# Attention matmuls of one 128-block: 128 streamed columns in place of 256 padded ones

## The chip, the cores and the metric

The kernel runs on one core of a Trainium2 chip. The metric is the device time of one execution in microseconds, the median over several runs; less is better.

## The reference

A decoder trunk of two layers on one sequence of 512 tokens with 1024 features, in float32:

```python
for i in range(DEPTH):                       # 2 layers
    hn = rmsnorm(h, norm_mix_g[i])
    h = h + (even_mixer if i % 2 == 0 else odd_mixer)(hn, ...)
    hn = rmsnorm(h, norm_mlp_g[i])
    u = jnp.square(jax.nn.relu(hn @ w_mlp_up[i]))      # 1024 -> 4096
    h = h + u @ w_mlp_down[i]
    gate = jax.nn.sigmoid(rmsnorm(h, norm_ple_g[i]) @ w_ple_gate[i])
    h = h + (p[i] @ w_ple_proj[i]) * gate
return rmsnorm(h, final_norm_g)
```

The even layer has 8 stick-breaking heads of width 64 and 4 differential heads, each with two score maps and values of width 128. The odd layer has 16 heads of width 64 with dilated windows. All are causal: a query attends to keys at or before it. The change touches only the two products of attention, `scores = q k^T` and `out = weights v`.

## The kernel before

Tokens are kept along the free axis (512 columns), features along the 128 partitions. To keep float32 accuracy with the rounded type `F32R`, most operands are held as a rounded part and its remainder, and most products are done as three matmuls, `mm3` at L129 to L131: high x high, low weights x high, high weights x low. Each matmul loads 128 columns of weights (in the profile LDWEIGHTS on PEld) and streams the other operand (MATMUL on PE).

The mixer of a layer works on groups of heads. While the projections of the next group run on PE (`project`, `lin_units`), the attention of the current group is fed in by steps (`attend`, `step`, `interleave`). For a head and a query block `i` (128 queries, 4 blocks), a step does

- `scores` (L479): two matmuls at L484 and L485 into a tile `sc` of which there are two, over the keys 0 to `n`, with the queries as the weights; the second uses `klz`, the keys' low part;
- `soft` (L494), or sigmoids and a running product for stick-breaking (L554 to L564), on DVE and ACT;
- `transpose_in` (L506), three steps later: it transposes `i + 1` blocks of weights on PE (L510) and writes them to `pth` (rounded, ACT, L514) and `ptl` (remainder, DVE, L515).

When the four query blocks of a head are done, `combine` calls `pv` (L517), the value products: for each key block `j` two matmuls (three in differential heads), with the values as weights, streaming the attention weights of the queries from `P * j` on.

`pth` and `ptl` have 13 slots of 128 columns. Slot `3 * j + i` holds the weights of key block `j` and query block `i`, so those of key block `j` start at slot `4 * j` and end with slot `3 * j + 3`. Key block 3 has one query block, slot 12. Before the change its product streams slots 11 and 12, and slot 11 is kept at zero: it is cleared once in each layer by GpSimd (L367). Likewise the scores of query block 0 need 128 keys, and `scores` streams 256. The further 128 columns are not read by anything.

The order of the work on each engine is set by a scheduler from its own costs of the instructions and from the dependences, so a change of shapes can also move instructions. Tiles that are used in turn (`sc` 2, `tp` 2, `pv` 1) set what waits for what.

Of the kernel before, what the change touches and what calls it, by code (L numbers as in the profile page):

```python
# [12 lines left out]
F32 = mybir.dt.float32  # L13
# [6 lines left out]
P = 128  # L20
# [42 lines left out]
def trunk(  # L63
# [5 lines left out]
    nc = tc.nc  # L69
    uid = [0]  # L70

    def nm(s):
        uid[0] += 1
        return f"{s}_{uid[0]}"
# [21 lines left out]
    def ps(tag):  # L96
        return psum.tile([P, S], F32, tag=tag, name=nm(tag), bufs=PS_BUFS[tag])
# [262 lines left out]
    def mixer(layer, norm, nxt):  # L360
# [2 lines left out]
        NSLOT = 13  # L363
        pth = [mpool.tile([P, NSLOT, P], F32R, tag=f"pth{i}", name=nm("pth"), bufs=1) for i in range(2)]
        ptl = [mpool.tile([P, NSLOT, P], F32R, tag=f"ptl{i}", name=nm("ptl"), bufs=1) for i in range(2)]
        for t in pth + ptl:
            nc.gpsimd.memset(t[:, 11, :].bitcast(F32), 0.0)  # L367
        pt_i = [0]

        ahl = norm.parts()  # L370
# [107 lines left out]

        def scores(hd, i):  # L479
            q, kh, kl = hd  # L480
            n = max(256, P * (i + 1))
            sp = ps("sc")
            qs = slice(i * P, (i + 1) * P)
            nc.tensor.matmul(sp[:, 0:n], q[:, qs], kh[:, 0:n], start=True, stop=False)  # L484
            nc.tensor.matmul(sp[:, 0:n], q[:, qs], kl[:, 0:n], start=False, stop=True)  # L485
            return sp
# [7 lines left out]
        def soft(hd, bt, i):  # L494
            n = P * (i + 1)
            sp = scores(hd, i)
            e = t2k("e")
            mn, s, r = col("mn"), col("s"), col("r")
            nc.vector.tensor_tensor_reduce(  # L499
                e[:, 0:n], sp[:, 0:n], bt[:, 0:n][:, ::-1], op0=ALU.add, op1=ALU.min,  # L500
                scale=1.0, scalar=3e38, accum_out=mn)
            nc.scalar.activation(e[:, 0:n], e[:, 0:n], AF.Exp, scale=-1.0, bias=mn, accum_out=s)  # L502
            nc.vector.reciprocal(r, s)
            return e, r
# [12 lines left out]
        def pv(parts):  # L517
            op = ps("pv")
            nmm = len(parts) * QT
            c = 0  # L520
            for j in range(QT):
                s0, q0 = (11, 256) if j == 3 else (4 * j, P * j)
                for stat, pt in parts:
                    mov = pt[:, s0:3 * j + 4, :].rearrange("p a b -> p (a b)")
                    nc.tensor.matmul(op[:, q0:S], stat(j), mov, start=c == 0, stop=c == nmm - 1)  # L525
                    c += 1
            return op

        def attend(g, kind, v, heads):
# [6 lines left out]
            def weights(x, i):  # L536
                n = P * (i + 1)
                if kind == "diff":
                    if i == 0:
                        slot = 8 + 2 * (2 * (g - 2) + x)  # L540
                        bias[x] = [load_bias(slot + m) for m in range(2)]
                    e0, r0 = soft(heads[2 * x], bias[x][0], i)
                    e1, r1 = soft(heads[2 * x + 1], bias[x][1], i)
                    nc.vector.tensor_scalar(e1[:, 0:n], e1[:, 0:n], r1, neglam, op0=ALU.mult, op1=ALU.mult)
                    nc.vector.scalar_tensor_tensor(
                        e0[:, 0:n], e0[:, 0:n], r0, e1[:, 0:n], op0=ALU.mult, op1=ALU.add)
                    return e0
                if kind == "dil":
                    if i == 0:
                        bias[x] = load_bias(4 * g + x)  # L550
                    e, r = soft(heads[x], bias[x], i)
                    nc.vector.tensor_scalar(e[:, 0:n], e[:, 0:n], r, None, op0=ALU.mult)
                    return e
                sp = scores(heads[x], i)  # L554
                dg = slice(i * P, (i + 1) * P)
                nc.vector.tensor_tensor(sp[:, dg], sp[:, dg], sbmask, op=ALU.add)
                e = t2k("e")
                kp = t2k("e")
                nc.scalar.activation(e[:, 0:n], sp[:, 0:n], AF.Sigmoid)
                sg = nc.scalar.activation(kp[:, 0:n], sp[:, 0:n], AF.Sigmoid, scale=-1.0)  # L560
                sig_tail[:] = [sg.ins]
                kr = kp[:, 0:n][:, ::-1]
                nc.vector.tensor_tensor_scan(kr, kr, kr, 1.0, op0=ALU.mult, op1=ALU.bypass)  # L563
                nc.vector.tensor_tensor(e[:, 0:n - 1], e[:, 0:n - 1], kp[:, 1:n], op=ALU.mult)  # L564
                return e

            def combine(x):
                hi, lo = pth[pts[x]], ptl[pts[x]]
                if kind == "diff":
                    vh = lambda j: v[:, j, P * x:P * x + P]  # L570
                    vl = lambda j: v[:, j, 256 + P * x:256 + P * x + P]
                    op = pv([(vh, hi), (vh, lo), (vl, hi)])
                    o = oT[2 * g + x]
                    nc.scalar.activation(o, op, AF.Copy)
                    return
                vs = lambda j: v[:, j, P * x:P * x + P]
                op = pv([(vs, hi), (vs, lo)])
                a = slice(64 * (x % 2), 64 * (x % 2) + 64)
                b = slice(64 - 64 * (x % 2), 128 - 64 * (x % 2))
                o = oT[2 * g + x // 2]  # L580
                nc.scalar.activation(o[a], op[b], AF.Copy)
                nc.vector.tensor_tensor(o[a], op[a], o[a], op=ALU.add)
# [208 lines left out]
    for layer in range(DEPTH):  # L791
        n_mlp, n_ple, n_next = Norm(1, layer), Norm(2, layer), Norm(0, layer + 1)
        mixer(layer, norm, n_mlp)
        with tc.tile_pool(name=f"ppool{layer}", bufs=1) as ppool:
            lo_eng[0] = nc.vector
            pj = ple_proj(layer, ppool)
            with tc.tile_pool(name=f"fpool{layer}", bufs=1) as fpool:
                mlp(layer, fpool, n_mlp, n_ple)
            with tc.tile_pool(name=f"gpool{layer}", bufs=1) as gpool:
                if layer < DEPTH - 1:  # L800
                    ple_t(layer, gpool, pj, n_ple, n_next)
                else:
                    ple_final(layer, gpool, pj, n_ple)
        norm = n_next
        lo_eng[0] = nc.gpsimd
# [77 lines left out]
```

## Time and profile before

| What | us |
|---|---|
| Median of 3 runs | 1341.06 |
| Fastest and slowest run | 1340.65, 1341.84 |
| Profiled execution, its own time | 1337.92 |
| Its span, first to last instruction | 1336.1 |
| PE busy in the span | 1300.5 |
| PEld (weight loads) busy | 1088.8 |
| DVE busy | 817.4 |
| ACT busy | 632.2 |
| POOL busy | 164.4 |

The granted TensorE clock was 0.998 over the span. Names in the profile are those of the program: `sc<-kh,qq` is a score matmul, `pv<-pth,v` a value product, `tp<-ident,e` a transpose, and `L484` the line in the kernel. A row of a group has the count, the busy time in us, the mean duration in ns, then the idle time before. Matmuls overlap in the records, so that their durations add up to more than the time they hold the engine.

### The profile page before, as it was taken

How to read it: one execution, taken by the hardware profiler on the slowest of the kernel's cores; microseconds unless marked ns; L12 is line 12 of the kernel's file. 1: busy time of each engine (PE TensorE's matmuls, PEld its weight loads, DVE VectorE, ACT ScalarE, POOL GpSimd, SP SyncE). 2: the span in 40 equal slices, each digit the busy share in tenths (PEclk: the TensorE clock that was granted, in tenths of full speed). 3: DMA queues.
4: the chain of work that ended last, by engine and by line, in shares of the span. 5: the costliest groups of instructions: out<-in, count | busy, mean ns of one | idle time of the engine just before them, and what ended most of it. 6: DMA issues, size and time to landing. Idle time of an engine off the chain costs nothing.

```text
span 1336.1 us, 16330 instructions
## 1 busy us (share of the span) xinstructions
PE 1300.5 (97%) x6360; PEld 1088.8 (81%) x6360; DVE 817.4 (61%) x1389; ACT 632.2 (47%) x1085; POOL 164.4 (12%) x90
## 2 busy tenths in 40 slices
PE   8999999899999999999999999999999999999997
PEld 6878777688888888888888898888888888888886
DVE  6788789865344344345667888887644434434566
ACT  5576758554223232233456666775422313324344
POOL 2322332310000000000003222221000000000001
PEclk9999999999999999999999999999999999999999
DMA  6321322243233222222232232213322232322221
GB/s 217 109 89 56 119 87 103 88 158 98 101 104 104 98 95 95 95 95 95 95 119 87 76 112 74 72 64 133 119 95 95 98 103 103 105 96 95 95 79 64
DMA packets 28030, 133.06 MB, mean 100 GB/s; under 512 B 3312, under 2 KB 4048, under 8 KB 15280
## 3 DMA queue, kind: packets, MB, share of 16 engines
q1 hardware_dynamic: 27952, 132.01, 29.0%
q8 instruction: 50, 0.82, 0.2%
q14 instruction: 28, 0.23, 0.1%
HBM read 125.63 MB, written 6.37 MB: 99 GB/s over the span
## 4 chain that ended last, share of the span: by engine, by line
PE 75%; DVE 14%; ACT 7%; issue 2%; DMA 0%; SPq 0%; ACTq 0%
PE mm L130 11%; PE mm L129 11%; PE mm L131 11%; PE tp L129 5%; PE tp L131 5%; PE tp L130 5%; PE sc L129 5%; PE sc L131 5%; PE sc L130 5%; PE pv L130 2%; PE pv L129 2%; PE pv L131 2%; DVE qq L458 2%; DVE e L563 2%; PE pv L525 2%
## 5 line engine op out<-in xcount | busy, mean ns | idle before, releaser
L120 ACT ACTIVATE wh<-raw 128x1024 fp32r<-128x1024 f32 (+1 forms) x216 | 224.7, 1043 | 496.8 <-PE mm L130 178.4
L129 PE MATMUL mm<-hi,wh 128*128 128x512 f32 x564 | 226.2, 401 | 0.5 <-ACT hi L169 0.5
L130 PE MATMUL mm<-lo,wh 128*128 128x512 f32 x564 | 220.5, 391 | 0.6 <-DVE lo L170 0.6
L131 PE MATMUL mm<-hi,wl 128*128 128x512 f32 x564 | 220.4, 391 | 0.3 <-DVE wl L121 0.3
L121 DVE TENSOR_TENSOR wl<-raw,wh 128x1024 fp32r<-128x1024 f32 x150 | 183.4, 1224 | 44.1 <-ACT wh L120 37.8
L121 POOL TENSOR_TENSOR wl<-raw,wh 128x1024 fp32r<-128x1024 f32 (+1 forms) x66 | 153.8, 2331 | 348.7 <-ACT wh L120 320.6
L131 PEld LDWEIGHTS mm<-hi,wl 128*128 128x128 f32 x564 | 105.9, 188 | 23.4 <-DVE wl L121 0.8
L129 PEld LDWEIGHTS mm<-hi,wh 128*128 128x128 f32 x564 | 106.2, 188 | 21.3 <-ACT hi L169 1.3
L130 PEld LDWEIGHTS mm<-lo,wh 128*128 128x128 f32 x564 | 106.2, 188 | 20.2 <-DVE lo L170 1.3
L502 ACT ACTIVATE e<-e,mn 128x128 f32<-128x128 f32 (+3 forms) x96 | 53.9, 561 | 51.5 <-DVE mn L499 50.8
L130 PE MATMUL mm<-ul,wh 128*128 128x512 f32 x192 | 74.7, 389 | 0.0
L131 PE MATMUL mm<-uh,wl 128*128 128x512 f32 x192 | 74.7, 389 | 0.0
L129 PE MATMUL mm<-uh,wh 128*128 128x512 f32 x192 | 74.7, 389 | 0.0
L131 PE MATMUL sc<-hi,wl 128*128 128x512 f32 x168 | 65.6, 390 | 0.0
L130 PE MATMUL sc<-lo,wh 128*128 128x512 f32 x168 | 65.4, 389 | 0.0
L129 PE MATMUL sc<-hi,wh 128*128 128x512 f32 x168 | 65.4, 389 | 0.0
L129 PE MATMUL mm<-wh,hi 128*128 128x256 f32 (+1 forms) x216 | 65.4, 303 | 0.0
L130 PE MATMUL mm<-wl,hi 128*128 128x256 f32 (+1 forms) x216 | 64.1, 297 | 0.4 <-DVE wl L121 0.4
L131 PE MATMUL mm<-wh,lo 128*128 128x256 f32 (+1 forms) x216 | 63.8, 295 | 0.0
L675 DVE TENSOR_TENSOR h<-h,mm 128x512 f32<-128x512 f32 x24 | 16.5, 688 | 72.7 <-PE mm L131 72.7
L129 PE MATMUL tp<-hi,wh 128*128 128x512 f32 x152 | 59.1, 389 | 0.0
L130 PE MATMUL tp<-lo,wh 128*128 128x512 f32 x152 | 59.1, 389 | 0.0
(218 smaller groups left out, 2835.1 us busy)
## 6 DMA issues: line engine op xcount, KB each, us to landing
raw<-in_w_up_dram SPq DMA_DIRECT2D x32, 1024.0 KB, 4.9
raw<-in_w_down_dram SPq DMA_DIRECT2D x32, 1024.0 KB, 4.9
raw<-in_w_in_dram SPq DMA_DIRECT2D x23, 1024.0 KB, 4.9
raw<-in_w_gate_dram SPq DMA_DIRECT2D x8, 1024.0 KB, 4.9
bias<-urow SPq DMA_DIRECT2D x24, 256.0 KB, 3.2
raw<-in_w_outa_dram SPq DMA_DIRECT2D x8, 768.0 KB, 4.3
pjd<-tmp SPq DMA_DIRECT2D x16, 256.0 KB, 2.2
pj<-pjd SPq DMA_DIRECT2D x16, 256.0 KB, 4.8
```

The lines of the kernel that those rows point to most:

```text
L120: nc.scalar.activation(hi, src, AF.Copy)
L121: lo_eng[0].tensor_tensor(lo, src, hi.bitcast(F32), op=ALU.subtract)
L129: nc.tensor.matmul(acc, lh, rh, start=start, stop=False)
L130: nc.tensor.matmul(acc, lh, rl, start=False, stop=False)
L131: nc.tensor.matmul(acc, ll, rh, start=False, stop=stop)
L458: nc.vector.tensor_tensor(q[b], f[a], q[a].bitcast(F32), op=ALU.subtract)
L502: nc.scalar.activation(e[:, 0:n], e[:, 0:n], AF.Exp, scale=-1.0, bias=mn, accum_out=s)
L525: nc.tensor.matmul(op[:, q0:S], stat(j), mov, start=c == 0, stop=c == nmm - 1)
L563: nc.vector.tensor_tensor_scan(kr, kr, kr, 1.0, op0=ALU.mult, op1=ALU.bypass)
L675: nc.vector.tensor_tensor(h[2 * c + i], h[2 * c + i], acc, op=ALU.add)
```

## The change

Scores of query block 0 stream their 128 keys. The value product of key block 3 streams slot 12 alone into the last 128 columns of `pv`. Slot 11 is no longer used, and its clearing is gone.

```diff
         ptl = [mpool.tile([P, NSLOT, P], F32R, tag=f"ptl{i}", name=nm("ptl"), bufs=1) for i in range(2)]
-        for t in pth + ptl:
-            nc.gpsimd.memset(t[:, 11, :].bitcast(F32), 0.0)
         pt_i = [0]
...
             q, kh, kl = hd
-            n = max(256, P * (i + 1))
+            n = P * (i + 1)
             sp = ps("sc")
...
             for j in range(QT):
-                s0, q0 = (11, 256) if j == 3 else (4 * j, P * j)
+                s0, q0 = 4 * j, P * j
                 for stat, pt in parts:
```

Two lines go, so that lines behind L366 have numbers lower by two in the changed kernel.

PE in layer 1, the end of a head: the first scores of the next head, two transposes, and the value products. Before:

```order
L484 MATMUL sc_6382<-kh_5887,qq_5844 128x256
L485 MATMUL sc_6382<-klz_179,qq_5844 128x256
L510 MATMUL tp_6393<-ident,e_6304 128x128 x2
L525 MATMUL pv_6398<-pth_5698,v_5713 128x512
L525 MATMUL pv_6398<-ptl_5700,v_5713 128x512
L525 MATMUL pv_6398<-pth_5698,v_5713 128x384
L525 MATMUL pv_6398<-ptl_5700,v_5713 128x384
L525 MATMUL pv_6398<-pth_5698,v_5713 128x256
L525 MATMUL pv_6398<-ptl_5700,v_5713 128x256
L525 MATMUL pv_6398<-pth_5698,v_5713 128x256
L525 MATMUL pv_6398<-ptl_5700,v_5713 128x256
L129 MATMUL mm_6238<-hi_5601,wh_6233 128x512
```

The same place now:

```order
L482 MATMUL sc_6374<-kh_5879,qq_5836 128x128
L483 MATMUL sc_6374<-klz_179,qq_5836 128x128
L508 MATMUL tp_6385<-ident,e_6296 128x128 x2
L523 MATMUL pv_6390<-pth_5694,v_5705 128x512
L523 MATMUL pv_6390<-ptl_5696,v_5705 128x512
L523 MATMUL pv_6390<-pth_5694,v_5705 128x384
L523 MATMUL pv_6390<-ptl_5696,v_5705 128x384
L523 MATMUL pv_6390<-pth_5694,v_5705 128x256
L523 MATMUL pv_6390<-ptl_5696,v_5705 128x256
L523 MATMUL pv_6390<-pth_5694,v_5705 128x128
L523 MATMUL pv_6390<-ptl_5696,v_5705 128x128
L129 MATMUL mm_6230<-hi_5597,wh_6225 128x512
```

Nothing moved here; four matmuls have half the columns, and the second score matmul has a transpose behind it.

PE in layer 0, scores of the second query block of two maps of a differential head, between matmuls of a projection (`mm`). Before:

```order
L129 MATMUL mm_543<-wh_667,hi_166 128x256
L130 MATMUL mm_543<-wl_668,hi_166 128x256
L131 MATMUL mm_543<-wh_667,lo_167 128x256
L129 MATMUL mm_543<-wh_667,hi_170 128x256
L484 MATMUL sc_599<-kh_351,qq_335 128x256
L485 MATMUL sc_599<-klz_176,qq_335 128x256
L130 MATMUL mm_543<-wl_668,hi_170 128x256
L131 MATMUL mm_543<-wh_667,lo_171 128x256
L129 MATMUL mm_543<-wh_667,hi_158 128x256
L130 MATMUL mm_543<-wl_668,hi_158 128x256
L131 MATMUL mm_543<-wh_667,lo_159 128x256
L129 MATMUL mm_543<-wh_667,hi_162 128x256
```

The same place now:

```order
L129 MATMUL mm_539<-wh_663,hi_166 128x256
L482 MATMUL sc_595<-kh_347,qq_331 128x256
L483 MATMUL sc_595<-klz_176,qq_331 128x256
L130 MATMUL mm_539<-wl_664,hi_166 128x256
L131 MATMUL mm_539<-wh_663,lo_167 128x256
L129 MATMUL mm_539<-wh_663,hi_170 128x256
L130 MATMUL mm_539<-wl_664,hi_170 128x256
L131 MATMUL mm_539<-wh_663,lo_171 128x256
L129 MATMUL mm_539<-wh_663,hi_158 128x256
L130 MATMUL mm_539<-wl_664,hi_158 128x256
L131 MATMUL mm_539<-wh_663,lo_159 128x256
L482 MATMUL sc_605<-kh_351,qq_334 128x256
```

The first pair stands three matmuls earlier; the second pair, which followed `hi_162` before, stands one earlier.

## The prediction

> **What bounds the kernel now.** I read the page's busy shares first, then its chain, then the busy time by stretch.
>
> ```profile
> span 1336.1 us, 16330 instructions
> PE 1300.5 (97%) x6360; PEld 1088.8 (81%) x6360; DVE 817.4 (61%) x1389; ACT 632.2 (47%) x1085; POOL 164.4 (12%) x90
> PE 75%; DVE 14%; ACT 7%; issue 2%; DMA 0%; SPq 0%; ACTq 0%
> ```
>
> PE is busy for 97% of the span and carries 75% of the chain that ended last, so a PE nanosecond is worth looking at. The busy time of PE overstates its work, since matmuls are pipelined; what counts is the distance from one matmul's start to the next one's, which I call its slot. The changed matmuls stand in the attention stretches only:
>
> ```profile
> 50.00:115.00 65.00, 60.26 (x373) 52.35 (x371) 51.41 (x134) 40.67 (x91) 18.93 (x8) 1.00 0.28 88
> 115.00:270.00 155.00, 144.74 (x759) 119.13 (x758) 131.73 (x234) 105.06 (x216) 51.57 (x22) 1.00 0.27 94
> 270.00:705.00 435.00, 435.00 (x1919) 359.83 (x1917) 217.33 (x265) 163.22 (x213) 10.25 (x8) 1.00 0.30 104
> 722.00:910.00 188.00, 184.27 (x1088) 161.24 (x1087) 156.80 (x399) 128.04 (x291) 53.59 (x24) 1.00 0.26 85
> ```
>
> Each row gives the stretch, its length, and then the busy time of PE, PEld, DVE, ACT and POOL. In the three attention stretches (first, second and last row) PE is busy for 60.26 + 144.74 + 184.27 = 389.27 of 408 us, which is 95%. Elsewhere it is solid. So I let 95% of any time that PE gains or loses here reach the end.
>
> **The change, part by part.** The groups by line and shape show how many matmuls of 256 columns there are:
>
> ```profile
> L484 PE MATMUL sc<-kh,qq 128*128 128x256 f32 x64 | 18.6, 292 | 2.9 <-DVE mn L499 1.8 <-DVE v L422 0.9
> L485 PE MATMUL sc<-klz,qq 128*128 128x256 f32 x64 | 18.0, 282 | 0.0
> L525 PE MATMUL pv<-pth,v 128*128 128x256 f32 x64 | 15.9, 281 | 0.0
> L525 PE MATMUL pv<-ptl,v 128*128 128x256 f32 x56 | 14.7, 281 | 0.0
> ```
>
> Half of each group is a block that needs 256 columns (the second query block, the third key block); the other half is padding to 256. So 32 + 32 + 32 + 28 = 124 matmuls go from 256 to 128 columns. What is a slot of 256 columns worth? The timeline of the last value products says it:
>
> ```profile
> 907.65 0.39 PE L525 MATMUL pv<-ptl,v 128*128 128x512 f32 x1
> 907.87 0.33 PE L525 MATMUL pv<-pth,v 128*128 128x384 f32 x1
> 908.04 0.34 PE L525 MATMUL pv<-ptl,v 128*128 128x384 f32 x1
> 908.22 0.28 PE L525 MATMUL pv<-pth,v 128*128 128x256 f32 x1
> 908.22 0.19 PEld L525 LDWEIGHTS pv<-ptl,v 128*128 128x128 f32 x1
> 908.34 0.28 PE L525 MATMUL pv<-ptl,v 128*128 128x256 f32 x1
> 908.46 0.28 PE L525 MATMUL pv<-pth,v 128*128 128x256 f32 x1
> 908.58 0.29 PE L525 MATMUL pv<-ptl,v 128*128 128x256 f32 x1
> 908.70 0.40 PE L129 MATMUL mm<-hi,wh 128*128 128x512 f32 x1
> ```
>
> Columns are start, duration, engine, line. Slots: 0.22 us at 512 columns (907.65 to 907.87), 0.175 at 384 (907.87 to 908.22, two), 0.12 at 256 (908.22 to 908.70, four). That is a straight line, some 0.055 us for 128 columns, and it would reach 0.06 at 128. But no matmul can start before its weights are in, and the weight load of the next one begins when the current one starts (PEld at 908.22 beside PE at 908.22). How long a load takes by itself shows where PE had been idle:
>
> ```profile
> 105.19 0.19 PEld L484 LDWEIGHTS sc<-kh,qq 128*128 128x128 f32 x1 [2.06 <-DVE mn L499]
> 105.19 0.39 PE L484 MATMUL sc<-kh,qq 128*128 128x256 f32 x1 [1.85 <-DVE mn L499]
> 105.30 0.19 PEld L485 LDWEIGHTS sc<-klz,qq 128*128 128x128 f32 x1
> 105.42 0.28 PE L485 MATMUL sc<-klz,qq 128*128 128x256 f32 x1
> 872.50 0.19 PEld L484 LDWEIGHTS sc<-kh,qq 128*128 128x128 f32 x1 [1.70 <-DVE mn L499]
> 872.61 0.19 PEld L485 LDWEIGHTS sc<-klz,qq 128*128 128x128 f32 x1
> ```
>
> The first matmul is recorded at 105.19 with 0.39 us where its group has 0.29: it really begins 0.11 later, when its weights are in, and just then (105.30) the next load begins. At 872.50, where the matmul has 384 columns, the load again holds the port for 0.11. So a load of 128 columns of this type costs 0.11 us whatever the matmul streams, and at 256 columns (0.12) it is only just hidden. A matmul of 128 columns leaves the next load 0.06 to hide behind: its slot becomes 0.11, not 0.06. Saved: 0.01 us.
>
> A transpose loads faster:
>
> ```profile
> L484 PEld LDWEIGHTS sc<-kh,qq x128: 186/188/192, 50.1 to 898.1; 128*128 128x128 f32 x128
> L510 PEld LDWEIGHTS tp<-ident,e x280: 137/140/143, 59.3 to 904.4; 128*128 128x128 f32 x140
> ```
>
> Its load is 188 - 140 = 48 ns shorter, so it holds the port for about 0.06 us (an estimate: 0.11 less 0.048). A short matmul with a transpose right behind it can therefore get down to 0.06 and saves 0.06. In the changed program's PE order 19 of the 124 have a transpose next (all of them second score matmuls); 105 have another product.
>
> Sum: 105 x 0.01 + 19 x 0.06 = 1.05 + 1.14 = 2.2 us; 95% of it is 2.1. Ends of this term: nothing, if 0.12 is a floor that shorter streams don't lower, and 124 x 0.06 = 7.4 us, if loads stop mattering. I take 2.1, since the load's 0.11 is read directly from rows of the very matmuls that change.
>
> The memsets that go:
>
> ```profile
> L367 POOL MEMSET pth<- x4: 198/201/205, 3.9 to 689.8; 128x128 f32 x4
> 689.96 0.35 POOL L367 MEMSET ptl<- 128x128 f32 x2
> 696.70 2.43 POOL L121 TENSOR_TENSOR wl<-raw,wh 128x1024 fp32r<-128x1024 f32 x1 [6.39 <-ACT wh L120]
> ```
>
> Eight memsets (four of pth, as many of ptl), 0.2 us each, leave POOL. Behind them POOL waits 6.39 us for ACT before its next work, so this is worth nothing; ends 0 and 0.7 us. Without the cover POOL would be the one to wait for, and it isn't.
>
> The order moves in layer 0. The place in the changed order at which a pair of scores comes earlier is this in the trace of before:
>
> ```profile
> 55.40 0.08 DVE L499 DVE_READ_ACCUMULATOR2_ANT mn<- 128x1 f32 x1
> 56.09 0.28 PE L129 MATMUL mm<-wh,hi 128*128 128x256 f32 x1
> 57.05 0.28 PE L129 MATMUL mm<-wh,hi 128*128 128x256 f32 x1
> 57.11 0.08 DVE L499 DVE_READ_ACCUMULATOR2_ANT mn<- 128x1 f32 x1
> 57.24 0.19 PEld L484 LDWEIGHTS sc<-kh,qq 128*128 128x128 f32 x1
> ```
>
> The first pair (behind the matmul at 56.09) comes three matmuls, 0.36 us, earlier; its buffer was free at 55.48, so PE doesn't wait. The second pair already waited for DVE (57.19, load at 57.24); one place earlier it waits up to 0.12 us more, and the projection matmuls queued behind it wait along. Such shifts help some scores and hurt others. I put this at 0, with ends of -1.5 and +1.5 us (a dozen such places at 0.12, an estimate from the changed order).
>
> Scores of the first block also end 0.05 us earlier for DVE. Those who waited for the second score matmul:
>
> ```profile
>   DVE e L499: 0.5, 2
>   DVE sc L556: 0.3, 1
> ```
>
> That is 0.8 us over all blocks; ends 0 and 0.8, and I take 0.
>
> The profiled execution took 1337.92 us (span 1336.1), the runs' median is 1341.06: 3.1 us apart, with the same work. The sum gives 1335.8 for the former, and 1341.06 - 2.1 = 1339.0 for the median, which I predict. 0.2% of it, 2.7 us, is about what a measurement of this kernel can tell from no change.
>
> A rule of the Trainium skill goes further than these rows. "TensorE: Matmul & The Clock Gate", section "Back-to-back issue gap", gives about 81 ns per matmul for a sustained stream of load and matmul pairs at 128 columns. By it the gain would be 124 x (0.12 - 0.081) x 0.95 = 4.6 us and the time 1336.5 (an estimate from that page). The same page's section on the weight path says that the fast weight load is off for FP32 input; the loads here read as f32, and no run here shows another type. The measured 0.11 decides for me.
>
> **The rivals.**
>
> *Short rounded products run slowly (slower).* No matmul of this type with fewer than 256 columns is in the trace; the only short products of plain FP32 are these:
>
> ```profile
> 48.37 0.39 PE L316 MATMUL sc<-e 32*16 32x128 f32 x2 [1.93 <-DVE v L422]
> L316 PE MATMUL sc<-e x2: 268/273/278, 48.4 to 48.5; 32*16 32x128 f32 x2
> ```
>
> One instruction leaves two entries, 0.39 - 0.27 = 0.12 us apart: 0.24 for 128 columns, four times what the line gives. If the engine treats a short rounded product in that way, each of the 124 slots goes to between 0.22 (the slot of 512 columns) and 0.24, and the cost is 124 x 0.105 x 0.95 = 12.4 to 14.1 us: 1353.5 to 1355. For it: the type is a fast form of FP32, and nothing here proves that it is fast at every length. Against it: from 512 to 256 columns the slots lie on one line, and the changed program has one matmul for each product as before. It decides for slower from a slot of 0.12 + 2.7/124 = 0.142 us. In a sentence of its own: "FP8 and Floating Point Precision" of the Trainium skill, section "TensorE Precision Notes", says that true FP32 takes four passes and the reduced form reads four bytes and truncates; it names no length at which the one becomes the other.
>
> *Streams decide, loads don't (faster).* The slot falls along the line to 0.06: 124 x 0.06 x 0.95 = 7.0 us, 1334.0. For it: the 19 places ahead of a transpose. Against it: the 0.11 of the isolated loads, and that each load begins no earlier than the matmul ahead of it.
>
> *Nothing at all.* 0.12 is a floor for a pair of load and matmul, or the gain lies where PE waits anyway: 1341.
>
> **How the numbers follow.** Loads bound the short slots, between nothing and a little over 3 us gained (1337.5 to 1341.1): 0.68, of which 0.12 beyond 0.2% faster, 0.04 slower by the order's shifts, and 0.52 within. Slow short products: 0.22. Streams alone, in full or for the most part: 0.10. So faster 0.12 + 0.10 = 0.22, same 0.52, slower 0.04 + 0.22 = 0.26. The range runs from 1336, which leaves out the stream case in full (about 0.08), to 1355, the upper end of the slow case.
>
> **What the profile after would show.** Right: the 124 matmuls of 128 columns start 0.11 us before the product behind them, 0.06 before a transpose; loads still 188 ns; PE's waits for DVE about as many. Wrong: slots of 0.22 or more, or two entries for each; or 0.06 to 0.08 everywhere; or the same slots and a different time, from waits that the new order of layer 0 makes.

## The result, and the profile after

The changed kernel is slower: 1343.82 us in the median of 15 runs (1341.58 to 1346.23), against 1341.01 us of 15 runs of the kernel before beside it (1337.66 to 1342.69). The ratio is 1.0026, with a 95% interval from 1.0018 to 1.0035. I had predicted 1339.0. The profiled execution took 1342.06 us, against 1337.92 before; each lies near the fast end of its runs, and these two differ by 4.1 us where the medians differ by 2.8.

The page of the changed kernel, its span, its busy shares and its chain:

```profile
span 1340.3 us, 16319 instructions
...
PE 1300.7 (97%) x6360; PEld 1087.6 (81%) x6360; DVE 819.6 (61%) x1389; ACT 631.6 (47%) x1085; POOL 162.4 (12%) x82
...
PE 74%; DVE 16%; ACT 7%; issue 2%; DMA 0%; SPq 0%; ACTq 0%
```

PE is busy as long as before, and the span grew by 4.2 us: so PE idles more. DVE's share of the chain went from 14% to 16%.

The slots first. The timeline of the last value products, the place that the prediction read:

```profile
912.45 0.19 PEld L523 LDWEIGHTS pv<-pth,v 128*128 128x128 f32 x1
...
912.56 0.23 PE L523 MATMUL pv<-pth,v 128*128 128x128 f32 x1
...
912.57 0.19 PEld L523 LDWEIGHTS pv<-ptl,v 128*128 128x128 f32 x1
...
912.63 0.27 PE L523 MATMUL pv<-ptl,v 128*128 128x128 f32 x1
...
912.68 0.19 PEld L129 LDWEIGHTS mm<-hi,wh 128*128 128x128 f32 x1
...
912.74 0.44 PE L129 MATMUL mm<-hi,wh 128*128 128x512 f32 x1
```

The two short products start 0.07 us apart, but they end at 912.79 and 912.90: 0.11 apart, like the loads (912.45, 912.57, 912.68). So the starts, by which the prediction wanted to see 0.11, do not show the slot of a short product; ends and loads do. From end to end, the median over the 28 pairs of short value products is 0.110 us where it was 0.118. Each product leaves one entry. The rival of slow short products is out.

So where do 4.2 us come from? Both traces hold 6360 matmuls, so the k-th of one can be laid beside the k-th of the other. Up to 53 us the changed kernel is level; it loses 0.87 us from 53 to 80 us, 2.74 us from 133 to 138 us and 0.42 us from there to 300 us; it gains 0.37 us in the attention of layer 1 (722 to 897 us) and loses 0.45 us between 897 and 910 us. The rest stays level. The largest step, in the timeline of the changed kernel (POOL, DVE, the ACT and PE rows that wait):

```profile
127.02 2.41 POOL L121 TENSOR_TENSOR wl<-raw,wh 128x1024 fp32r<-128x1024 f32 x1 [5.73 <-ACT wh L120]
...
127.56 0.16 DVE L501 RECIPROCAL r<-s 128x1 f32<-128x1 f32 x1
127.76 1.87 DVE L542 TENSOR_SCALAR e<-e,r,neglam 128x384 f32<-128x384 f32 x1
129.67 0.69 DVE L456 TENSOR_TENSOR qq<-tmp,qq 64x512 fp32r<-64x512 f32 x1
130.38 0.62 DVE L543 SCALAR_TENSOR_TENSOR e<-e,r,e 128x384 f32<-128x384 f32 x1
131.03 0.69 DVE L456 TENSOR_TENSOR qq<-tmp,qq 64x512 fp32r<-64x512 f32 x1
131.75 0.69 DVE L497 CUSTOM_DVE_ANT_0 e<-sc,bias 128x512 f32<-128x512 f32 x1
...
132.55 0.72 ACT L500 ACTIVATE e<-e,mn 128x512 f32<-128x512 f32 x1 [3.50 <-DVE mn L497]
...
133.39 0.17 DVE L501 RECIPROCAL r<-s 128x1 f32<-128x1 f32 x1 [0.74 <-ACT e L500]
133.47 0.67 DVE L497 CUSTOM_DVE_ANT_0 e<-sc,bias 128x512 f32<-128x512 f32 x1
...
136.87 0.50 PE L589 MATMUL pv<-tmp,ones_r 128*128 128x512 f32 x1 [2.26 <-ACT tmp L586]
```

The same place before:

```profile
125.01 2.41 POOL L121 TENSOR_TENSOR wl<-raw,wh 128x1024 fp32r<-128x1024 f32 x1 [4.29 <-ACT wh L120]
...
125.68 0.16 DVE L503 RECIPROCAL r<-s 128x1 f32<-128x1 f32 x1 [0.17 <-ACT e L502]
125.87 0.69 DVE L499 CUSTOM_DVE_ANT_0 e<-sc,bias 128x512 f32<-128x512 f32 x1
...
126.48 1.15 DVE L544 TENSOR_SCALAR e<-e,r,neglam 128x384 f32<-128x384 f32 x1
...
129.84 0.67 DVE L499 CUSTOM_DVE_ANT_0 e<-sc,bias 128x512 f32<-128x512 f32 x1
...
133.47 0.47 PE L591 MATMUL pv<-tmp,ones_r 128*128 128x512 f32 x1
```

Before, the score reduction (L499, now L497) stood right behind the RECIPROCAL. Now four instructions stand between them, and it comes 5.9 us later, of which 0.9 us is what PE had lost by then. ACT's exp waits 3.50 us for it, the next RECIPROCAL waits 0.74 us for that exp, and the second reduction follows at 133.47 us, 3.63 us later than before (129.84). PE, further down, waits 2.26 us for ACT; before, it did not wait at that matmul. From then on PE is behind by the same 3.63 us.

These 3.63 us have three parts. PE had lost 0.9 us by then. From the first RECIPROCAL to the second reduction it is now 5.91 us where it was 4.16, so 1.75 us are lost there. The remaining 1.0 us DVE had lost ahead of the RECIPROCAL, for the most part at an earlier TENSOR_SCALAR. It takes 1.62 us in the timeline of the changed kernel:

```profile
119.75 1.62 DVE L542 TENSOR_SCALAR e<-e,r,neglam 128x128 f32<-128x128 f32 x1
```

And in that of the kernel before, 0.77:

```profile
120.04 0.77 DVE L544 TENSOR_SCALAR e<-e,r,neglam 128x128 f32<-128x128 f32 x1
```

One of the four is odd: the TENSOR_SCALAR takes 1.87 us. The same form in the timeline of the kernel before, at another place, takes 0.48:

```profile
113.63 0.48 DVE L544 TENSOR_SCALAR e<-e,r,neglam 128x384 f32<-128x384 f32 x1
```

The long one ends at 129.63, 0.2 us after POOL's subtraction, which ends at 129.43. Before, it ended at 127.63 and POOL's subtraction at 127.42: the same 0.2 us. The earlier one, at 119.75 us, ends 0.1 us after the subtraction beside it in both kernels; in the changed kernel it begins 0.9 us behind POOL's start, before 2.0 us. The small loss in layer 1 shows this by itself. The timeline there before:

```profile
897.48 0.35 DVE L552 TENSOR_SCALAR e<-e,r 128x256 f32<-128x256 f32 x1
897.52 2.02 POOL L121 TENSOR_TENSOR wl<-raw,wh 128x768 fp32r<-128x768 f32 x1 [6.35 <-ACT wh L120]
...
898.67 0.62 ACT L502 ACTIVATE e<-e,mn 128x384 f32<-128x384 f32 x1 [0.17 <-ACT pth L514]
```

And of the changed kernel:

```profile
901.25 1.84 POOL L121 TENSOR_TENSOR wl<-raw,wh 128x768 fp32r<-128x768 f32 x1 [6.41 <-ACT wh L120]
...
901.34 1.90 DVE L550 TENSOR_SCALAR e<-e,r 128x256 f32<-128x256 f32 x1
...
903.81 0.61 ACT L500 ACTIVATE e<-e,mn 128x384 f32<-128x384 f32 x1 [1.67 <-DVE mn L497]
```

Where DVE begins 0.04 us ahead of POOL, DVE takes 0.35 us and POOL 2.02. Where POOL begins 0.09 us ahead, POOL takes 1.84 us and DVE 1.90. In these rows who comes first takes its usual time, and the other takes longer. The Trainium skill gives a rule for this in "SBUF — State Buffer", section "Who interferes with whom": GpSimd has no SBUF ports of its own but shares DVE's second pair, which is locked for a whole instruction by a `tensor_scalar` in a 2-port mode or by a GpSimd operation, while the other one stands still until the end. These rows agree. The same section lets DVE operations with at most one SBUF input, outside those modes, pass beside POOL; the reduction at 125.87 us, which reads PSUM and takes its usual 0.69 us while POOL runs, fits that.

At 897 us DVE's own sequence is the same in both kernels; its last changed place lies at 892 us. From there a shift of 0.13 us between DVE and POOL is enough to turn round who is first.

That is two theories for the loss: the order on the engines, as such; or the order together with POOL, which makes some of its late places dear. And as a rival of both: the short products themselves.

### The profile page after: what moved, and what is told of

It is laid out like the page before. It is cut to its first block, busy times and chain, and to the rows that moved or that the text cites. A ratio compares the mean times of both kernels' runs of the same rounds, so it can differ in the third digit from the quotient of the medians.

```text
span 1340.3 us, 16319 instructions
## 1 busy us (share of the span) xinstructions
PE 1300.7 (97%) x6360; PEld 1087.6 (81%) x6360; DVE 819.6 (61%) x1389; ACT 631.6 (47%) x1085; POOL 162.4 (12%) x82
## 4 chain that ended last, share of the span: by engine, by line
PE 74%; DVE 16%; ACT 7%; issue 2%; DMA 0%; SPq 0%; ACTq 0%
PE mm L129 11%; PE mm L130 11%; PE mm L131 11%; PE tp L130 5%; PE tp L131 5%; PE tp L129 5%; PE sc L130 5%; PE sc L131 5%; PE sc L129 5%; PE pv L130 2%; PE pv L131 2%; PE pv L129 2%; DVE qq L456 2%; DVE e L561 2%; DVE e L562 1%
## 5 line engine op out<-in xcount | busy, mean ns | idle before, releaser
L121 POOL TENSOR_TENSOR wl<-raw,wh 128x1024 fp32r<-128x1024 f32 (+1 forms) x66 | 153.0, 2319 | 764.3 <-ACT wh L120 741.0
L121 DVE TENSOR_TENSOR wl<-raw,wh 128x1024 fp32r<-128x1024 f32 x150 | 183.4, 1224 | 44.0 <-ACT wh L120 37.7
```

The lines of the kernel that those rows point to most:

```text
L121: lo_eng[0].tensor_tensor(lo, src, hi.bitcast(F32), op=ALU.subtract)
```

## Experiments

### The order and the shapes apart

In the first group each kernel has one side of the change. "Order held" means that the instructions of PE, DVE and ACT were chained, in the sequence of another kernel, by dependences between neighbours on an engine that wait for nothing:

```diff
+    for engine, runs in ORDERS.items():
+        own = [i for i in traced if str(i.engine).split(".")[-1] == engine and i.opcode in REAL]
...
+        seq = [own[k + off] for k, off in enumerate(at)]
+        for earlier, later in zip(seq, seq[1:]):
+            order(later, earlier)
```

`ORDERS` is a table of positions. The short products in the old order, and the padded products in the new one:

> All three edits of the change, with the order of every engine held to that of the kernel before. Order theory (the loss comes from the scheduler's new order in layer 0): 1 to 2 us faster than before, ratio 0.9985 to 0.9995, since only the shorter slots are left. Rival (short products themselves, or what they do to waits, cost the time): 2.5 to 4.5 us slower, ratio 1.002 to 1.0035, as the changed kernel.

> The kernel before, its padded matmuls and its memsets, with PE, DVE and ACT held to the order of the changed kernel. Order theory: 3.5 to 6 us slower than before, ratio 1.0026 to 1.0045 (the loss without the gain of the shorter slots). Rival (short products cost): ratio 0.999 to 1.001.

Measured: 1340.41 us for the shapes in the old order, ratio 1.0001 [0.9993, 1.0010]; 1344.62 us for the new order with the padded products, ratio 1.0038 [1.0026, 1.0051] (before: 1340.26). The loss is the order's, all of it. The gain of 1 to 2 us that I expected of the shapes is not there: the interval reaches from 0.9 us faster to 1.3 us slower.

Which of the two edits moves the order?

```diff
-            n = max(256, P * (i + 1))
+            n = P * (i + 1)
```

> Only the scores of the first query block stream 128 columns; the scheduler orders freely. Its order in layer 0 differs from before at the places at which the changed kernel lost 2.7 us (DVE between 110 and 132 us). Order theory: 2 to 4 us slower, ratio 1.0015 to 1.003. Rival (cost per short product, 64 of 124 here): half the loss, ratio 1.0013.

```diff
-                s0, q0 = (11, 256) if j == 3 else (4 * j, P * j)
+                s0, q0 = 4 * j, P * j
```

(without the memsets)

> Only the value products of the last key block stream 128 columns, memsets gone; the scheduler orders freely and moves only a few instructions, near 85 us. Order theory: between 1 us faster and 0.5 us slower, ratio 0.9992 to 1.0004. Rival (cost per short product, 60 of 124 here): ratio 1.0013.

Measured: the scores alone 1344.61 us, ratio 1.0046 [1.0031, 1.0062]; the value products alone 1340.57, ratio 1.0006 [0.9997, 1.0015]. The scores alone lose more than I expected (a ratio of 1.0030 at most), and the value products come out just above their range (1.0004 at most). The scheduler gives a score matmul of 128 columns another place: by the traces 58 places of DVE change with the scores alone, and 18 with the value products alone.

The table shows, for all kernels, what the k-th matmul's end gained (-) or lost (+) against the kernel before in each stretch, in us, from one profiled execution of each. An asterisk is a stretch of half TensorE clock (below); one such stretch adds some 1 to 2 us.

```
stretch of before, us     0-53    53-80   80-133  133-138  138-300  300-722  722-897  897-910
changed kernel           -0.01    +0.87    +0.03    +2.74    +0.42    -0.03    -0.37    +0.45
order_only               -0.37    +0.83    +0.07    +2.71    +0.53    +0.00    +0.01    +0.42
shapes_old_order         -0.12    +0.01   +1.41*    +0.01    -0.03    -0.01    -0.39    -0.02
scores_only              -0.22    +0.94    -0.59   +3.75*    -0.23    -0.03    -0.34    +0.51
values_only             +2.46*    -0.04    +0.60    +0.03    +0.66    -0.01    -0.03    -0.04
one_back                +1.65*    +0.88    -0.02    +1.28    +0.38    -0.03    -0.37    +0.42
one_forth              +2.07**    +0.01   +1.21*    +1.65    +0.09    -0.01    -0.01    +0.00
order_dve               +2.64*    +0.84   +1.94*    +0.04    +0.08    -0.03    -0.39    -0.02
order_pe               +4.08**    +0.01   +3.32*   +4.41*    -0.28    -0.02    -0.37    +0.47
layer1_only             +2.00*    +0.04   +1.18*    -0.01    +0.19    -0.01    -0.45    +0.48
half_stream             -0.12    +0.84    -0.02    +2.78    +0.41    -0.02    -0.41    +0.45
pieces_two               -1.21    +0.12    +0.58    +0.13    -2.64    -0.87    -1.53    +0.00
pieces_old               -3.17    +0.58    -1.94    +0.15    -4.65    -0.57    -4.39    +0.00
pieces_eight             -3.80    +1.13    -3.45    -0.31  -0.43**    -0.82    -4.42    +0.00
pieces_new               -2.52    +1.67   -0.62*   +3.36*   -5.30*    -0.59    -4.91    -0.02
pieces_shapes_old        -2.61    +0.66    -1.82    +0.16    -5.26    -0.59    -4.91    -0.02
```

The first two rows are nearly alike up to 722 us: the padded kernel in the new order loses what the changed one loses, stretch by stretch. The loss at 897 us stands in the rows of just those kernels whose DVE has the changed place at 892 us, as long as POOL subtracts in one piece.

### One instruction, one engine

Does the one late reduction make the jump? It was moved alone, in both directions, with the order of the other instructions as it was; here one place of DVE in the changed kernel:

```diff
 L501 RECIPROCAL
+L497 score reduction 128x512
 L542 TENSOR_SCALAR 128x384
 L456 qq
 L543 SCALAR_TENSOR_TENSOR 128x384
 L456 qq
-L497 score reduction 128x512
```

> The changed kernel, all its shapes and its order on PE, with one single instruction moved on VectorE: the 128x512 score reduction (L497) that stands behind two query scalings and two TENSOR_SCALARs at 131.75 us goes back to right behind the RECIPROCAL ahead of them, where the kernel before has it (125.87 us). Theory (this one late reduction makes the exp wait 3.50 us and PE 2.26 us): the jump between 133 and 138 us in the lag behind the kernel before, 2.7 us, goes; 1338.5 to 1341.5 us for a before of 1340.3, ratio 0.9995 to 1.0010. Rival A (the loss is spread over the hundred-odd moved places of layer 0, and this jump is only where it becomes visible): 0.5 us at most comes back, ratio 1.0020 to 1.0035. Rival B (the reduction was late because its scores were late, so moving it ahead makes DVE wait for them instead): slower than the changed kernel, ratio over 1.0035, with a DVE wait for sc of 2 us or more ahead of L497.

> The kernel before, with its padded products, its memsets and its order on PE and ACT, and one instruction moved on VectorE: the 128x512 score reduction (L499) at 125.87 us goes behind the four instructions that stand ahead of it in the changed kernel. Theory: this alone makes most of the loss; PE idles about 2 us more between 131 and 138 us and the time rises by 2 to 3 us, ratio 1.0015 to 1.0025. Rival A (the loss needs the whole new order): within 0.5 us, ratio 0.9995 to 1.0005. Theory that the short products have any part in it: they are absent here, so the rise would be missing.

Measured: back, 1342.68 us, ratio 1.0018 [1.0009, 1.0027]; forth, 1341.09 us, ratio 1.0008 [0.9999, 1.0017] (before: 1339.61). Neither size was met. In the table the jump falls from 2.74 to 1.28 us with the one instruction back, and moving it forth makes 1.65 us: it is the largest single part, a little over half. The other part is the earlier TENSOR_SCALAR of 128 columns: it takes 1.68 us with the instruction back, and 0.78 with it forth. From the first RECIPROCAL to the second reduction it is 4.5 us back and 5.8 us forth, where the kernel before needs 4.2, so going back removes most of the loss between the two and keeps the one ahead of them, and going forth makes the former without the latter. The rows of the kernel with the instruction back:

```profile
129.25 0.67 DVE L506 CUSTOM_DVE_ANT_0 e<-sc,bias 128x512 f32<-128x512 f32 x1
...
129.84 1.40 DVE L551 TENSOR_SCALAR e<-e,r,neglam 128x384 f32<-128x384 f32 x1
...
133.64 0.67 DVE L506 CUSTOM_DVE_ANT_0 e<-sc,bias 128x512 f32<-128x512 f32 x1
...
134.35 0.72 ACT L509 ACTIVATE e<-e,mn 128x512 f32<-128x512 f32 x1 [2.60 <-DVE mn L506]
```

Then whole engines: the changed kernel with DVE alone, or PE alone, held to the old order.

> The changed kernel with VectorE alone held to the order of the kernel before; TensorE and ScalarE keep what the changed kernel gives them, but for 15 matmuls. Theory (VectorE's order carries the loss): ratio 0.9990 to 1.0008. Rival (TensorE's order carries it, with pairs of scores and projections in other places): 1.0020 to 1.0040.

> The changed kernel with TensorE alone held to the order of the kernel before; VectorE keeps what the changed kernel gives it, but for 4 instructions. Theory (VectorE's order carries the loss): ratio 1.0018 to 1.0040, with the reduction L497 near 131 us and the exp behind it waiting over 3 us. Rival (TensorE's order carries it): 0.9990 to 1.0008.

Measured: DVE held, 1343.01 us, ratio 1.0017 [1.0008, 1.0026]; PE held, 1346.0 us, ratio 1.0048 [1.0034, 1.0061]. The first lies between the two expectations, the second above both, and the table says why. With DVE's old order the jump is gone (0.04), and so is the loss at 897 us; with PE's old order it is the loss at 53 to 80 us that is gone (0.01), and the jump stays. So DVE's order makes the losses at 133 and at 897 us, and PE's order the 0.8 us at 53 to 80. With PE held the median is the highest of all; in its profiled execution it has the most half-clock stretches. Some of ACT's places move too when one engine is held (16 of them with DVE), so the parting is not quite clean.

### What a short slot is

The value products of the last key block stream 64 columns instead of 128, in the changed kernel's order; half of the last query block's columns are left out for that key block:

```diff
-                    nc.tensor.matmul(op[:, q0:S], stat(j), mov, start=c == 0, stop=c == nmm - 1)
+                    n = S - q0 if j < 3 else 64
+                    nc.tensor.matmul(op[:, q0:q0 + n], stat(j), mov[:, 0:n], start=c == 0, stop=c == nmm - 1)
```

> The changed kernel in its own order, with the value products of the last key block streaming 64 columns instead of 128; it leaves out half of the last query block's columns of that key block. Theory (the weight load of 0.11 us bounds a short slot): the pairs of pth and ptl products still end 0.108 to 0.112 us apart, and the time stays within 1 us of the changed kernel's. Rival (streams decide, on a line of 0.12 us at 256 and 0.11 at 128): the distance falls to 0.08 to 0.10 us, and layer 1 becomes 0.5 us or more shorter.

Measured, from one execution: 1341.83 us, as against 1342.06 in the profiled one of the changed kernel. The rows:

```profile
912.39 0.20 PE L534 MATMUL pv<-pth,v 128*128 128x64 f32 x1
912.39 0.19 PEld L534 LDWEIGHTS pv<-ptl,v 128*128 128x128 f32 x1
912.42 0.27 PE L534 MATMUL pv<-ptl,v 128*128 128x64 f32 x1
912.50 0.19 PEld L139 LDWEIGHTS mm<-hi,wh 128*128 128x128 f32 x1
```

The loads are still 0.11 us apart, and the ends of a pair are 0.111 us apart in the median, as with 128 columns; layer 1 gains 0.41 us where it gained 0.37. Streaming half as much changes nothing: here the slot follows the loads, and not the stream.

Layer 1 alone with both edits (layer 0 as before, with its memsets):

```diff
-            n = max(256, P * (i + 1))
+            n = P * (i + 1) if layer else max(256, P * (i + 1))
...
-                s0, q0 = (11, 256) if j == 3 else (4 * j, P * j)
+                s0, q0 = (11, 256) if j == 3 and not layer else (4 * j, P * j)
```

> The short products of both kinds in layer 1 alone, where TensorE is busy all the time; layer 0 as in the kernel before, its memsets too. Theory (the slots give 8 ns each, 62 of them, some 30 ns more ahead of a transpose, and only layer 1 turns that into time; all of the loss is the order of layer 0): 0.3 to 0.7 us faster, ratio 0.9992 to 1.0002, and a lag of zero behind the kernel before up to 690 us. Rival A (the short products themselves cost time on the chip): ratio above 1.0010. Rival B (the prediction's 8 to 10 ns count in full everywhere, so half of 2.1 us is won here): ratio 0.9988 to 0.9995.

Measured: 1340.51 us, ratio 0.9998 [0.9989, 1.0007] (before: 1340.97). The ratio is in the range, but not for the reason I gave: it wins 0.45 us in layer 1 and loses 0.48 at 897 us, by the DVE row that stands behind POOL there. In its profiled execution, too, the short products and the order of layer 1 cancel.

### POOL's part

POOL makes the remainder `wl` of the weights with one long subtraction (L121, in `wsplit`). If its length is what DVE waits for, pieces must help, in the kernel before too. In four pieces (six where `wl` has 768 columns, which gives a step of 128):

```diff
-        lo_eng[0].tensor_tensor(lo, src, hi.bitcast(F32), op=ALU.subtract)
+        parts = 4 if lo_eng[0] is nc.gpsimd else 1
...
+                lo_eng[0].tensor_tensor(lo[at], src[at], hi.bitcast(F32)[at], op=ALU.subtract)
```

This moves no instruction of PE, DVE or ACT. Done in the changed kernel, in the kernel before, and with the short products in the old order:

> The changed kernel, with every POOL subtraction that makes wl (L121, 2.41 us at 128x1024) written as four or six pieces; the order on PE, DVE and ACT stays the changed kernel's. Port theory (the late reduction at 131.75 us is late because the TENSOR_SCALAR ahead of it takes 1.87 us instead of 0.42: it ends 0.2 us after the POOL subtraction beside it, as if POOL held what it needs; with pieces DVE gets its turn after 0.7 us at most): the long DVE operations shrink, DVE's time above the short form of each operation falls from 67 us to below 35, the jump of 2.7 us at 133 us falls to 1.5 or less, ratio 0.9970 to 1.0010. Order theory alone (the late place costs what it costs, POOL has no part in it): DVE durations as before, jump of 2.7 us, ratio 1.0020 to 1.0035.

> The kernel before with the same pieces on POOL and nothing else; its order on PE, DVE and ACT is unchanged. Port theory: the kernel before has 66 us of such long DVE operations too, those in layer 0 up to 260 us lie on the path in part: 1 to 5 us faster, ratio 0.9960 to 0.9993, and the gap between this kernel and the changed one with pieces is smaller than the 3.5 us without. Rival A (DVE waits just as long, since POOL takes the next piece at once): ratio 0.9995 to 1.0010. Rival B (the pieces make POOL late for PE, 0.1 us or more for each piece): slower, ratio above 1.0010, with PE waits for wl of L121.

> Short products of both kinds, the order of the kernel before on PE, DVE and ACT, and POOL's pieces: the version that should beat both kernels. Port theory: 0.4 us below the kernel before with pieces (what layer 1 gains from the short products), ratio 0.9955 to 0.9990. Rivals as for the kernel before with pieces: 0.9992 to 1.0007 if DVE waits just as long, above 1.0007 if POOL becomes late.

Measured, against 1341.19 us: changed kernel with pieces 1328.24 us, ratio 0.9904 [0.9890, 0.9919]; kernel before with pieces 1324.32, ratio 0.9876 [0.9860, 0.9893]; short products, old order and pieces 1323.33, ratio 0.9869 [0.9854, 0.9883]. The gain is several times what I expected, and the last version beats both kernels by over 1%. Of the 17 us that the kernel before gains, 14 stand between profiled executions without a half-clock stretch (1337.92 and 1323.92 us); the rest goes, at least in part, with the half clock, which the versions in the old order no longer meet with these pieces. To tell the length from other effects, two pieces and pieces of 128 columns (eight or six), in the kernel before:

```diff
-        lo_eng[0].tensor_tensor(lo, src, hi.bitcast(F32), op=ALU.subtract)
+        step = nk // 2 if lo_eng[0] is nc.gpsimd else nk
...
+        step, cols = (1, P) if lo_eng[0] is nc.gpsimd else (nk, n)
```

> The kernel before with POOL's wl subtraction in two pieces (128x512, 1.2 us each) instead of one; order unchanged. Port theory (POOL holds what DVE needs until its instruction ends, so the length of that instruction sets the price): DVE's time above the short forms between the 66 us of one piece and the 27 us of four, about 40 to 50, and 8 to 14 us faster than the kernel before, ratio 0.9895 to 0.9940. Rival (any break lets PE or DVE have wl early, and that is what helps): about the 16 us of four pieces, ratio 0.9870 to 0.9885. Rival (chance of phase between POOL and DVE, not the length): no order between one, two, four and eight pieces.

> The kernel before with POOL's wl subtraction in pieces of 128 columns (8 of 128x128, or 6 where wl has 768); order unchanged. Port theory: DVE's long operations shrink again (below 27 us in sum), but POOL pays a fixed 0.1 us or so for each piece; 16 to 19 us faster than the kernel before, ratio 0.9860 to 0.9882. Rival (POOL becomes late: its work grows from 160 to over 260 us): less than with four pieces, ratio above 0.9885, with PE waits for POOL's wl.

Measured, against 1340.20 us: two pieces 1335.92 us, ratio 0.9963 [0.9950, 0.9977]; eight 1326.25, ratio 0.9894 [0.9876, 0.9911]. In the kernel before DVE is busy for 817.4 us and POOL for 164.4. The busy shares on the page of two pieces:

```profile
PE 1299.9 (98%) x6360; PEld 1088.2 (82%) x6360; DVE 803.6 (60%) x1389; ACT 632.9 (48%) x1085; POOL 188.5 (14%) x156
```

Of four:

```profile
PE 1297.8 (98%) x6360; PEld 1088.5 (82%) x6360; DVE 785.0 (59%) x1389; ACT 632.5 (48%) x1085; POOL 229.7 (17%) x320
```

Of eight:

```profile
PE 1300.3 (98%) x6360; PEld 1092.9 (83%) x6360; DVE 775.6 (59%) x1389; ACT 633.1 (48%) x1085; POOL 272.4 (21%) x520
```

DVE runs the same 1389 instructions and gets shorter with every cut: by 13.8, 32.4 and 41.8 us. So DVE's time depends on the length of POOL's instruction. The kernel's time follows down to four pieces; two gave less than expected, 4.3 us. Eight gave 14 us where I expected 16 to 19: POOL's own time has grown by 108 us, and one wait of PE has grown. From the waits of PE with eight pieces (us in total, times, longest):

```profile
PE mm L133 <- ACT tmp L352: 3.5, 1, 3.5
```

In the timeline ACT itself waits there for a DMA that stores `tmp`:

```profile
155.57 0.60 ACT L352 ACTIVATE tmp<-mm 128x512 f32<-128x512 f32 x1 [4.44 <-DMA pjd<-tmp]
```

The same wait of PE, and that of transposes for DVE, with four:

```profile
PE mm L135 <- ACT tmp L354: 1.1, 1, 1.1
...
PE tp L516 <- DVE ptl L521: 1.0, 3, 0.5
```

The longest of PE's waits in the kernel before:

```profile
PE tp L510 <- DVE ptl L515: 6.9, 8, 1.4
```

The waits of transposes for DVE fall from 6.9 us to 1.0 with four pieces. No wait of 0.2 us or more of PE for POOL's `wl` stands in these views, with one piece or with four, so an earlier `wl` is not the gain. With eight, the trace names a store and not `wl`; whether POOL's longer work delays it was not tried.

Does POOL make the price of the new order? In part. At 897 us yes: with pieces the new order loses nothing there (-0.02 for 0.45). Of the jump, about 0.9 us: by 135 us, ahead of the half clock, it is 1.8 us where it was 2.7 (both from the k-th matmuls). Little of that comes from the TENSOR_SCALAR of 1.87 us. The changed kernel with pieces:

```profile
124.63 0.90 DVE L548 TENSOR_SCALAR e<-e,r,neglam 128x384 f32<-128x384 f32 x1
125.56 1.11 DVE L462 TENSOR_TENSOR qq<-tmp,qq 64x512 fp32r<-64x512 f32 x1
...
126.70 0.98 DVE L549 SCALAR_TENSOR_TENSOR e<-e,r,e 128x384 f32<-128x384 f32 x1
```

The first is 1.0 us shorter, but the next two, which took 0.69 and 0.62 us behind the long subtraction, now stand beside pieces and are stretched, and from the RECIPROCAL to the second reduction it is still 5.7 us. What the pieces win lies ahead of the RECIPROCAL: the TENSOR_SCALAR of 128 columns takes 0.71 us instead of 1.62. The rest stays with the place of the reduction behind the other instructions: in the old order with pieces it is 4.3 us from the RECIPROCAL to the second reduction. I had expected that the gap between the two orders would shrink, and it did not: 1328.24 - 1324.32 = 3.9 us in the medians, with three half-clock stretches in the profile of the one and none in that of the other.

## Why the prediction was wrong

- **Counts and slots: right.** 124 short matmuls, one entry each, bounded by the load at 0.11 us; half the columns again changed nothing. By ends the saving for most of them is some 0.01 us (0.118 to 0.110 between value products).
- **Ahead of a transpose: too much.** I took a slot of 0.06 us for the 19 second score matmuls, which saves 0.06, and 0.01 for the first ones. From the end of the matmul ahead of such a pair of scores to the end of the transpose behind it, where no wait intervenes, it is 0.307 or 0.308 us against 0.341 to 0.351 before. That is 0.03 to 0.04 us for both scores, not 0.07.
- **95% of PE's gain reaches the end: wrong in layer 0.** In the old order the short products gain 0.39 us in layer 1, by the scores (0.34 alone) and not by the value products (0.03 alone), and nothing in layer 0 (+0.01 at 53 to 80 us and at 133 to 138 us). Of 2.1 us, 0.4 were there, too little for the medians to show. PE's mean busy share of 95% doesn't tell which wait ends last: where PE waits for DVE, what it is early only makes that wait longer. That is my reading; why the value products of layer 1 give nothing was not traced.
- **The order: the step that failed.** I put it "at 0, with ends of -1.5 and +1.5 us (a dozen such places at 0.12, an estimate from the changed order)". It costs 0.9 + 2.7 + 0.4 + 0.45 us = 4.5 us in the profiled execution, where the short products gain 0.4. I priced moves of PE alone, by the length of a PE slot. The price was on DVE: 67 of its 1293 places changed, and one reduction fell behind four instructions of 0.48 to 0.69 us, one of them stretched to 1.87 us. The delay went on to ACT (a wait of 3.50 us) and to PE (2.26 us). An earlier TENSOR_SCALAR came nearer to the start of POOL's subtraction and took 1.62 us instead of 0.77. The prediction has no term for DVE's order, nor for what POOL does to DVE.
- **Memsets: right.** Without them, and in the old order, the time is the same.
- **The rivals.** Slow short products and streams that decide are both out; "the same slots and a different time, from waits that the new order of layer 0 makes" is what happened, and I had given it 0.04. (In the rival of slow products, a slot of 0.22 us costs 0.10 more than one of 0.12, not 0.105, so its lower end is 11.8 us and not 12.4.)

## What to carry to other kernels

When a shape changes under a scheduler, compare the order on every engine first, and price each moved instruction by what stands ahead of it now and who waits for it: here a saving of 0.01 us a matmul was paid with a reduction 5.9 us late. Look at the duration of one form over its places, not at the mean: a DVE operation of 0.48 us that takes 1.87 ends just after POOL's instruction beside it. Where POOL works beside a busy DVE, try shorter POOL instructions: four pieces instead of one took 17 us from this kernel, and eight were no better.

## What the runs showed of the hardware

**The half clock.** In some executions the granted clock falls to one half for 3.41 us, behind an idle time of PE. A window of the kernel with the short products in the old order (stretch, length; busy time of PE, PEld, DVE, ACT, POOL; then the clock, 0.50, and DMA):

```profile
105.60:108.60 3.00, 3.00 (x15) 3.00 (x14) 1.63 (x9) 0.60 (x2) 0.00 (x0) 0.50 0.00 0
```

And rows of its timeline, in this stretch and behind it:

```profile
105.11 0.38 PE L492 MATMUL sc<-kh,qq 128*128 128x256 f32 x1 [1.87 <-DVE mn L507]
...
105.84 0.42 PE L139 MATMUL mm<-wh,hi 128*128 128x256 f32 x1
106.06 0.41 PE L140 MATMUL mm<-wl,hi 128*128 128x256 f32 x1
...
109.34 0.28 PE L139 MATMUL mm<-wh,hi 128*128 128x256 f32 x1
109.46 0.28 PE L140 MATMUL mm<-wl,hi 128*128 128x256 f32 x1
```

A slot of 256 columns is 0.22 us in it and 0.12 behind it, and this stretch costs 1.4 us. The kernel before has the same idle time (1.85 us, at 103 us) and kept the full clock in its profile. The clock changes at multiples of 3.41 us from one another. I laid such a grid over the 17 profiled executions: a window of 3.41 us in which PE was idle for 0.52 or more was followed by a half-clock one 16 times, and not followed twice (0.55 both); below 0.52 it was followed four times, where two lows behind one another count once. So the share of idle time in a window tells most of these cases, not all. By it, whether one idle time of 1.9 us falls into one window or is cut by two decides over 1.4 us, and this goes with much of the scatter of these runs: of the kernel before, runs with a mean clock of 0.997 or more have a median of 1339.27 us, the others 1341.11 (34 and 48 runs). All eight runs with four pieces in the old order are at 0.997 or more. "TensorE: Matmul & The Clock Gate" of the Trainium skill, Part 1, tells of a free-running window of 3413 ns after which an idle engine gets half the clock; the length agrees, and here a little over half a window of idle time was mostly enough.

**Two readers of SBUF.** With POOL's long subtractions DVE is busy for 817.4 us, with the shortest ones for 775.6: over 40 us of what the page calls DVE's busy time was waiting.
